# Two feed-forwards whose high and low token parts share one 512-column product, and an expert stage with one more buffer, a regrouped gather and a branch that stands later

## The chip, the cores and the metric

The kernel runs on one core of a Trainium2 chip. The metric is the device time of one launch in microseconds (us); lower is better. A profiled execution leaves a trace, whose span is the time from its first to its last instruction.

## The reference, cut to what matters

256 tokens of width 1024 pass through two blocks, all in 32-bit floats. The part that matters here:

```python
def swiglu(x, w_gate, w_up, w_down):                      # hidden width 2816, twice in the first block
    return (jax.nn.silu(x @ w_gate) * (x @ w_up)) @ w_down

x = x + FFN_HALF * swiglu(rms_norm(x, norm_ffn1[l]), ffn1_gate[l], ffn1_up[l], ffn1_down[l])
...                                                       # stick-breaking attention and RWKV-7
x = x + FFN_HALF * swiglu(rms_norm(x, norm_ffn2[l]), ffn2_gate[l], ffn2_up[l], ffn2_down[l])
...                                                       # second block: context, differential attention, Fourier
def hier_moe(h, w_rg, b_rg, w_re, b_re, w1, w3, w2):      # 4 groups of 4 experts, the best 2 of one group
    g_sel = jnp.argmax(t @ w_rg + b_rg, axis=-1)
    ...
    y = (jax.nn.silu(t @ w1e) * (t @ w3e)) @ w2e          # for each expert, times its gate
```

## The kernel before, in words

The program has five stages: feed-forward 1, the mixing of the first block, feed-forward 2, the projections and attention of the second block, and the 16 experts. Engines run their own queues in program order: PE (TensorE) multiplies, ACT (ScalarE) and DVE (VectorE) work between, POOL does small things, SP issues the weight loads. Outside the stretches marked `manual_schedule` a scheduler decides the order in each queue by priority; inside them it is the order in which the code is written.

**Feed-forwards.** To keep the accuracy of 32-bit floats with fast products, every weight and every token value is split into a high and a low part. A load brings 1 MB (`raw`, 128 x 2048); `split_w` makes from each half of it `hi` (ACT, L262) and `lo` (DVE, L263), three buffers of each. `swiglu` runs over 11 chunks of 256 hidden columns. In each, `fm256` forms the gate and then the up product: for two halves f of 128 columns and 8 pieces k of the width, three products into the same 256 columns of a PSUM bank: high weights by high tokens (L226), high weights by low tokens (L227), low weights by high tokens (L228). A chunk has 4 x 8 such threes, both feed-forwards 704. The bank with both halves is read once: silu (L618), multiplication (L619), splitting (L518, L519). Then `down256` multiplies the chunk before with 24 products of 512 columns (L403, L404, L407) into four banks that collect the result. Banks of the kind `pa` are four, taken in turn.

**Experts.** `x_add`, `x_turn`, `x_high` and `logits` form the residual, its transpose, the high part of the normalized tokens and the router's 20 logits for each block b of 128 tokens. `x_low(b)` (DVE) makes the low parts, and `pick(b)` (eight small DVE operations) chooses the group and its two experts. `rank` products number the tokens of each expert, `one_hot` makes selection matrices, and `gather(p)` multiplies them with the tokens for a pair p of experts (`gat`, L1799); DVE writes the result scaled to `xe` (L1800). There are 8 pairs; each has three products with 4 MB of weights: `gate(p)`, `up(p)` and `down(p)`, all at L1832. The order on PE is gate(p), down(p-1), up(p), sometimes gather(p+1), `back(p)`, the adding back of pair p-1 to the tokens, and the transposes `hidden_T(p)` (`eT`). Behind gate(0) `places()` forms the gates' slots (`gsl`).

The weights of the experts are 96 loads of 1 MB. `load_rows` deals them out in turn over 13 buffers: 5 `rawa`, 4 `raw`, 4 `rawb`. SP issues them in one queue and waits for a buffer to come free. An expert has 64 places; if any token finds none, `overflow()` computes all experts densely in a branch (`tc.If`, L1904) that every engine must decide. Here no token overflows, and the branch is skipped. SP's way around the branch waits until all loads issued so far have landed. In the kernel before the branch stands behind pair 6, and the loads (7,0), (6,2) and (7,1) are issued ahead of it, where (p,i) is the product i (0 gate, 1 up, 2 down) of pair p; (7,2) follows it.

Of the kernel before, what the change touches and what calls it, by code (L numbers as in the profile page):

```python
# [33 lines left out]
def constants():  # L34
# [57 lines left out]
    nm=17, m1=4,  # L92
# [5 lines left out]
    ffn={"4": 16, "2": 11, "1": 2, "m": 12},  # L98
    mid={"r4": 9, "r2": 6, "r1": 7, "rm": 16, "v4": 3, "s4": 6, "sm": 6, "gm": 4, "m2": 2, "mm": 2, "pm": 4, "cm": 4, "c1": 2},
    blk={"4": 9, "2": 5, "1": 7, "m": 25}, att={"4": 6, "2": 9},  # L100
    moe={"4": 4, "xe": 2, "oh": 2, "h": 3, "1": 2, "m": 16}, raws=(5, 4, 4))
# [16 lines left out]
def _body(tc, nc, es, I, out, dbg, stop, R):  # L118
# [36 lines left out]
    def t4(name, dt=F32, tag=None):  # L155
        return alloc("4", 1024, name, dt, tag)

# [127 lines left out]
    def fm256(w, c0, h, l, nk=8, wk=None, ps=None):  # L285
# [8 lines left out]
        return ps  # L294

# [150 lines left out]
    H = [cp.tile([128, 1024], F32R, name=f"H{i}") for i in range(4)]  # L446
    K4 = [cp.tile([128, 1024], F32, name=f"K{i}") for i in range(4)]
# [36 lines left out]

    def hl(name, tag=None):
        if tag == "H":
            h, l = H[0:2], H[2:4]
        else:
            h = [t4(name + "h", F32R, tag) for _ in range(2)]
            l = [t4(name + "l", F32R, tag) for _ in range(2)]  # L490
        v = lambda ts: (lambda k: ts[k // 4][:, 256 * (k % 4):256 * (k % 4) + 256])
        return v(h), v(l)
# [5 lines left out]
    def trans_split(xn, sc, bias, name, tag=None):  # L498

        h, l = hl(name, tag)  # L500
# [14 lines left out]
        return h, l  # L515
# [5 lines left out]
    def lead(xs, src, nk, n, sc, bias=None, evac=None, fk=0):  # L521


        h, l = hl("", "H")
# [65 lines left out]
        return h, l, lambda: picker(ws, n), lambda: picker([ws1, split_w(raw1, 1)], n)  # L590

    def swiglu(xs, g, wg, wu, wd, pre=None):

        if pre:
            h, l, w0, w1 = pre
            yield
        else:
            xn = normed(xs, "xn")
            yield
            h, l = trans_split(xn, g, None, "hT")  # L600
# [9 lines left out]
        for j in range(nch):  # L610
            if j == 2 and c1dma:
                c1dma()
            pg = fm256(wg, 256 * j, h, l, 8, w0)
            pu = fm256(wu, 256 * j, h, l, 8, w1)
            w0 = w1 = None
# [120 lines left out]
    def context_steps():  # L736
# [3 lines left out]
        h, l = hl("", "H")  # L740
# [29 lines left out]
    def context_values(n):  # L770
        h, l = hl("", "H")
# [17 lines left out]
    M["hT"], M["lT"], w0, w1 = lead(x, [I["w_in"][:, c:c + 256] for c in FIRST], 8, 256, gain("nm"), None, M["evac"])  # L789
# [594 lines left out]
    hT, lT, *w0 = lead(x, [w2i[512 * i:512 * i + 512, 1024:1536] for i in range(2)], 4, 512, col(sc1), col(sh1), M["evac"])  # L1384
# [86 lines left out]
    heads = [t4("heads") for _ in range(2)]  # L1471
# [14 lines left out]
    def attention():  # L1486
# [47 lines left out]
        def turn(n):  # L1534
# [6 lines left out]
            h_, l_ = t4("aTh", F32R), t4("aTl", F32R)  # L1541
# [30 lines left out]
    yF = [t4("yF") for _ in range(2)]  # L1572
# [87 lines left out]
    yh, yl = hl("y2", "H")  # L1660
# [15 lines left out]
    pl = pa("lgp")  # L1676
    route = tc.manual_schedule(engines={mybir.EngineType.DVE, mybir.EngineType.Activation})
# [38 lines left out]
    def logits(b):  # L1716
        for k in range(8):
            mm(pl[:, 32 * b:32 * b + 20], xT[b][:, 128 * k:128 * k + 128], wr[:, k, :], start=k == 0, stop=k == 7)
# [7 lines left out]
    def pick(b):  # L1726
        DVE.scalar_tensor_tensor(L[:, b], pl[:, 32 * b:32 * b + 20], rsx[:, b:b + 1], rbias, op0=OP.mult, op1=OP.add)
        v = L[:, b].rearrange("p (g e) -> p g e", g=5)
        vi, vj = v[:, :, :, None].to_broadcast([128, 5, 4, 4]), v[:, :, None, :].to_broadcast([128, 5, 4, 4])
        gt, eq = (t1(n)[:, 0:80].rearrange("p (g i j) -> p g i j", g=5, i=4) for n in ("gt", "eq"))  # L1730
        tri = C("tri").rearrange("p (i j) -> p i j", i=4)[:, None].to_broadcast([128, 5, 4, 4])
# [4 lines left out]
        DVE.tensor_reduce(rk[:, b], gt, axis=AX.X, op=OP.add)  # L1736
        DVE.tensor_scalar(sel[:, b], rk[:, b, 0], 0.0, None, op0=OP.is_equal)
# [342 lines left out]
```

## Time and profile before

| | |
|---|---|
| Time, median of 3 runs (lowest to highest) | 1179.94 us (1179.67 to 1182.61) |
| The profiled execution's own time | 1180.25 us |
| Its span | 1178.5 us, so 1.75 us lie around it |
| PE busy | 1108.8 us, 94% of the span |
| DVE, ACT busy | 621.2 us (53%), 477.3 us (40%) |
| Moved from memory | 262.98 MB, 223 GB/s in the mean |

PE is busy nearly everywhere; the loads are light at first (about 190 GB/s in the feed-forwards) and at the limit near the end (420 GB/s). A shorter time can so come from less work on PE in the first part and from an earlier, denser stream of loads in the last. Matmuls overlap in the records: the cost of one is the distance from its start to the next one's start, not its recorded duration.

### The profile page before, as it was taken

To read this page: it belongs to the slowest core of one execution; us is meant where nothing else is said; L and a number is where in the kernel's file an instruction comes from. 1 tells how busy PE (TensorE), PEld (TensorE's weight loads), DVE (VectorE), ACT (ScalarE), POOL (GpSimd) and SP (SyncE) were. 2 spreads that over 40 slices of the span, in tenths; PEclk is the share of its full clock that TensorE was granted. 3 is DMA by queue.
4 is the path that set the end of the run, shared out by engine and by line. 5 is a ranking of instruction groups with operands and counts; after the bars stand their busy time and mean duration, and the time that the engine had idled before them with its cause. 6 is when DMAs were issued, how large, how long until landed. Compare 5 with 4: busy or idle time off the path is not lost. (4 is left out here: it accounts for less than half of the span.)

```text
span 1178.5 us, 17991 instructions
## 1 busy us (share of the span) xinstructions
PE 1108.8 (94%) x7527; PEld 870.1 (74%) x7527; DVE 621.2 (53%) x928; ACT 477.3 (40%) x711; POOL 60.7 (5%) x106
## 2 busy tenths in 40 slices
PE   6999999998988999999999999999899799999976
PEld 6999997887756888999998688888898534343432
DVE  4545545556976556455445865666656603232314
ACT  5444444476643355444444445555544300100002
POOL 1000001000330001000000100000000200000000
PEclk9999999999988999999999999999999799999988
DMA  9855654453557548555556454214285399999984
GB/s 338 275 191 179 198 180 158 157 169 112 179 197 261 197 139 304 195 179 185 175 191 218 153 179 160 72 55 152 96 327 210 145 366 419 421 420 420 421 354 175
DMA packets 119538, 262.98 MB, mean 223 GB/s; under 512 B 6873, under 2 KB 83802, under 8 KB 105242
## 3 DMA queue, kind: packets, MB, share of 16 engines
q1 hardware_dynamic: 118506, 258.88, 60.7%
q0 software_dynamic: 656, 2.36, 0.6%
q8 instruction: 61, 1.00, 0.3%
q10 hardware_dynamic: 288, 0.52, 0.1%
q14 instruction: 27, 0.22, 0.1%
HBM read 260.70 MB, written 1.05 MB: 222 GB/s over the span
## 5 line engine op out<-in xcount | busy, mean ns | idle before, releaser
L263 DVE TENSOR_TENSOR lo<-raw,hi 128x1024 fp32r<-128x1024 f32 x243 | 297.2, 1224 | 285.9 <-ACT hi L262 285.5
L262 ACT ACTIVATE hi<-raw 128x1024 fp32r<-128x1024 f32 x246 | 260.6, 1060 | 318.2 <-PE pj L227 203.3
L227 PE MATMUL pj<-H,hi 128*128 128x256 f32 x752 | 212.4, 283 | 4.1 <-issue 4.1
L226 PE MATMUL pj<-H,hi 128*128 128x256 f32 x752 | 216.2, 288 | 0.0
L228 PE MATMUL pj<-H,lo 128*128 128x256 f32 x752 | 212.4, 282 | 0.4 <-POOL lo L263 0.4
L226 PEld LDWEIGHTS pj<-H,hi 128*128 128x128 f32 x752 | 142.8, 190 | 8.5 <-issue 4.5
L228 PEld LDWEIGHTS pj<-H,lo 128*128 128x128 f32 x752 | 143.0, 190 | 5.2 <-issue 4.5
L227 PEld LDWEIGHTS pj<-H,hi 128*128 128x128 f32 x752 | 142.7, 190 | 1.3 <-issue 0.5
L228 PE MATMUL pj<-hTh,lo 128*128 128x256 f32 x352 | 99.4, 283 | 0.1
L227 PE MATMUL pj<-hTl,hi 128*128 128x256 f32 x352 | 99.2, 283 | 0.0
L226 PE MATMUL pj<-hTh,hi 128*128 128x256 f32 x352 | 99.1, 283 | 0.0
L227 PEld LDWEIGHTS pj<-hTl,hi 128*128 128x128 f32 x352 | 67.3, 192 | 1.3 <-DVE hTl L509 0.8
L226 PEld LDWEIGHTS pj<-hTh,hi 128*128 128x128 f32 x352 | 67.2, 192 | 1.2 <-ACT hTh L508 0.8
L228 PEld LDWEIGHTS pj<-hTh,lo 128*128 128x128 f32 x352 | 67.4, 192 | 0.3 <-DVE lo L263 0.3
L1881 DVE TENSOR_TENSOR yf<-yacc,K 128x512 f32<-128x512 f32 x16 | 11.0, 691 | 104.7 <-PE yacc L1832 82.5
L404 PE MATMUL acc<-lo,hTh 128*128 128x512 f32 x160 | 63.1, 394 | 0.0
L403 PE MATMUL acc<-hi,hTh 128*128 128x512 f32 x160 | 62.7, 392 | 0.0
L407 PE MATMUL acc<-hi,hTl 128*128 128x512 f32 x160 | 49.9, 393 | 0.0
L1832 PE MATMUL pu<-rawa,xe 128*64 128x512 f32 x160 | 45.3, 605 | 0.0
L1864 ACT ACTIVATE hT<-eT 128x512 f32<-128x512 f32 x8 | 4.8, 597 | 91.6 <-PE eT L1863 91.6
L1832 PE MATMUL pg<-raw,xe 128*64 128x512 f32 x128 | 35.8, 595 | 0.0
L1832 PE MATMUL yacc<-rawb,hT 128*64 128x512 f32 x128 | 35.5, 592 | 0.0
(496 smaller groups left out, 1895.2 us busy)
## 6 DMA issues: line engine op xcount, KB each, us to landing
raw<-in_w_in_dram SPq DMA_DIRECT2D x43, 1024.0 KB, 5.1
raw<-in_ffn_up_dram SPq DMA_DIRECT2D x22, 1024.0 KB, 5.2
raw<-in_ffn_down_dram SPq DMA_DIRECT2D x22, 1024.0 KB, 4.9
raw<-in_ffn_gate_dram SPq DMA_DIRECT2D x21, 1024.0 KB, 5.2
rawa<-in_w_exp_up_dram SPq DMA_DIRECT2D x20, 1024.0 KB, 19.2
raw<-in_w_exp_gate_dram SPq DMA_DIRECT2D x16, 1024.0 KB, 14.1
rawb<-in_w_exp_down_dram SPq DMA_DIRECT2D x16, 1024.0 KB, 17.5
raw<-in_w_mod_dram SPq DMA_DIRECT2D x15, 1024.0 KB, 5.0
```

Of the source, the lines that this page charges most:

```text
L226: mm(o, l[0], r[0], start=first, stop=False)
L227: mm(o, l[0], r[1], start=False, stop=False)
L228: mm(o, l[1], r[0], start=False, stop=last)
L262: ACT.activation(hi, r, AF.Copy)
L263: low = lambda: (sub or DVE).tensor_tensor(lo, r, f32(hi), op=OP.subtract)
L403: mm(ps[b][n], hh, wh[:, s_], start=first and f == 0, stop=False)
L404: mm(ps[b][n], hh, wl[:, s_], start=False, stop=False)
L407: mm(ps[b][n], ll, wh[:, s_], start=False, stop=last and f == 1)
L1832: mm(o[halves[u]], l[:, 64 * u:64 * u + 64], r[u], start=first, stop=last, tile_position=(0, 64 * u))
L1864: ACT.activation(t, ps, AF.Copy)
L1881: tt(part(yf, n), yaccs[p][n], part(g2b, n), op=OP.mult)
```

## The change

The feed-forwards place the high and the low tokens behind one another in one tile (`H`, or two `t8` tiles), so that one product of 512 columns with the high weights (L308) gives both halves of a whole bank; a product of 256 columns with the low weights (L311) adds to its first half. The two halves of the bank are then added by ACT (copy) and DVE (addition), for each f apart, before silu and the multiplication. Ahead of the experts the picks of both blocks become one with operations twice as wide, `x_low(1)` moves behind the first one-hots, `gather(0)` goes over four banks, high parts first, then low, and ACT shares the scaling; PE's order there is the written one. The tiles K0 and K1 become one that serves as a 14th buffer for expert weights. The loads (7,2) are issued ahead of the branch, and the branch stands behind hidden_T of pair 7. The last `down` does its first half of the data in the common order and its second half by column half. `few` in the skipped branch loads from ACT's queue.

```diff
-    raws=(5, 4, 4))
+    raws=(5, 4, 4, 1))
@@ load_rows
+        elif i == sum(n) - 1:
+            raw = K01
+    def fm128s(w, c0, hl2, wk=None):
+        wk = wk() if wk else cols(w, c0, 256, 0, 8)
+        for f in range(2):
+            ps, s_ = pa("pj"), slice(128 * f, 128 * f + 128)
+            for k in range(8):
+                wh, wl = wk(k)
+                high = lambda: mm(ps, wh[:, s_], hl2(k), start=k == 0, stop=k == 7)
+                if k < 7:
+                    high()
+                mm(ps[:, 0:256], wl[:, s_], hl2.h(k), start=False, stop=False)
+                if k == 7:
+                    high()
+            yield ps[:, 0:256], ps[:, 256:512]
@@ swiglu
-            pg = fm256(wg, 256 * j, h, l, 8, w0)
-            pu = fm256(wu, 256 * j, h, l, 8, w1)
-            ACT.activation(hp, pg, AF.Silu)
-            tt(hp, hp, pu, op=OP.mult)
-            split2(hT[0], hT[1], hp)
+            for s_, (a, b) in zip(sides, fm128s(wg, 256 * j, hl2, w0)):
+                t = t1("gs")
+                ACT.activation(t, a, AF.Copy)
+                tt(t, t, b, op=OP.add)
+                ACT.activation(hp[:, s_], t, AF.Silu)
+            for s_, (a, b) in zip(sides, fm128s(wu, 256 * j, hl2, w1)):
+                t, o = t1("us"), hp[:, s_]
+                ACT.activation(t, a, AF.Copy)
+                tt(t, t, b, op=OP.add)
+                tt(o, o, t, op=OP.mult)
+                split2(hT[0][:, s_], hT[1][:, s_], o)
@@ routing
     x_low(0)
-    pick(0)
-    x_low(1)
-    pick(1)
+    pick()
@@
     for b in range(2):
         one_hot(b, 0, 4)
+    x_low(1)
@@ gather
+        if p == 0:
+            pss = pc2("gat") + pc2("gat")
+            for i in range(2):
+                for k in range(8):
+                    sums(pss[k // 2], k, i, i == 0 and k % 2 == 0, i == 1)
+            for k in range(8):
+                if k % 2:
+                    ACT.activation(g(k), half(pss[k // 2], k), AF.Identity, bias=sh2p[:, k:k + 1], scale=sc2p[:, k:k + 1])
+                else:
+                    DVE.tensor_scalar(g(k), half(pss[k // 2], k), sc2p[:, k:k + 1], sh2p[:, k:k + 1], op0=OP.mult, op1=OP.add)
+            for b in range(2):
+                one_hot(b, 4, 12)
+            return
@@ down
         if p == 7:
-            steps.sort(key=lambda v: v[1])
+            steps[4:] = [(2, 0), (3, 0), (2, 1), (3, 1)]
@@ the pairs
             hTs[p] = hidden_T(hps[p], alloc("h", 512, "hT", F32, ""))
-            if p == 6:
-                ahead.update({k: fetch(*k) for k in ((7, 0), (6, 2), (7, 1))})
+            if p == 7:
+                ahead[7, 2] = fetch(7, 2)
                 overflow()
```

On PE, in the first chunk of feed-forward 1, a stretch of the queue reads so before (`H_78`, `H_79` are high tokens, `H_80`, `H_81` low ones, `hi` and `lo` the weights):

```order
L226 MATMUL pj<-H_78,hi 128x256
L227 MATMUL pj<-H_80,hi 128x256
L228 MATMUL pj<-H_78,lo 128x256
L226 MATMUL pj<-H_79,hi 128x256
L227 MATMUL pj<-H_81,hi 128x256
L228 MATMUL pj<-H_79,lo 128x256
```

and so now:

```order
L308 MATMUL pj<-H,hi 128x512
L311 MATMUL pj<-H,lo 128x256
L308 MATMUL pj<-H,hi 128x512
L311 MATMUL pj<-H,lo 128x256
L308 MATMUL pj<-H,hi 128x512
```

Of each three rows two remain, with as many columns in all.

On DVE, from the end of the logits to the first results of the gather, before (`H_81<-x_72` is x_low(1), `m` the picks, `oh` the one-hots; the six rows of each pick between its first and last are left out):

```order
L1727 SCALAR_TENSOR_TENSOR L<-lgp,rsx,rbias 128x20
...
L1738 SCALAR_TENSOR_TENSOR m_8820<-rk,sel 128x16
L1713 SCALAR_TENSOR_TENSOR H_81<-x_72,rsx,H_79 128x512 x2
L1727 SCALAR_TENSOR_TENSOR L<-lgp,rsx,rbias 128x20
...
L1738 SCALAR_TENSOR_TENSOR m_8820<-rk,sel 128x16
L1773 TENSOR_TENSOR oh<-c_67,rank 128x256 x2
L1780 COPY pr_8933<-rank 128x32
L1800 TENSOR_SCALAR xe<-gat,sc2p,sh2p 128x256 x2
```

and now:

```order
L1765 SCALAR_TENSOR_TENSOR L<-lgp,rsx,rbias 128x20 x2
L1771 TENSOR_TENSOR gt<-L 128x160
...
L1778 SCALAR_TENSOR_TENSOR m_8504<-rk,sel 128x16 x2
L1811 TENSOR_TENSOR oh<-c_67,rank 128x256 x2
L1750 SCALAR_TENSOR_TENSOR H<-x_72,rsx,H 128x512 x2
L1819 COPY pr_8609<-rank 128x32
L2035 RECIPROCAL den<-den 128x2
L1850 TENSOR_SCALAR xe<-gat,sc2p,sh2p 128x256 x4
```

x_low(1) has moved from between the picks to behind the one-hots, one pick is gone, and the reciprocal of the gates now stands ahead of the gather's results.

On SP, the end of the queue of loads before (the rows of the skipped branch are left out):

```order
L245 DMA rawb<-in_w_exp_up_dram 128x2048 x3
L245 DMA rawa<-in_w_exp_up_dram 128x2048
L1903 TENSOR_LOAD novi
L1904 COMPARE_AND_BRANCH
...
L1904 UNCONDITIONAL_BRANCH x2
L1903 ISA x2
L245 DMA rawa<-in_w_exp_down_dram 128x2048 x4
```

and now:

```order
L250 DMA rawa<-in_w_exp_up_dram 128x2048
L250 DMA raw<-in_w_exp_up_dram 128x2048 x3
L250 DMA raw<-in_w_exp_down_dram 128x2048
L250 DMA rawb<-in_w_exp_down_dram 128x2048 x3
L1960 TENSOR_LOAD novi
L1961 COMPARE_AND_BRANCH
```

The last four loads of weights have moved from behind the branch to ahead of it.

## Rows read from the trace of the kernel before

**Rows 1.** The page's first line.

```profile
span 1178.5 us, 17991 instructions
```

**Rows 2.** Busy time by stretch, in feed-forward 1: us, then PE, PEld, DVE, ACT, POOL, clock, DMA.

```profile
100.00:150.00 50.00, 50.00 (x357) 47.11 (x356) 24.79 (x25) 21.97 (x24) 0.00 (x0) 1.00 0.58 190
```

**Rows 3.** Timeline of PE in one chunk: start us, duration us, engine, line, operation.

```profile
99.80 0.28 PE L226 MATMUL pj<-H,hi 128*128 128x256 f32 x1
...
105.14 0.39 PE L403 MATMUL acc<-hi,hTh 128*128 128x512 f32 x1
...
110.61 0.28 PE L226 MATMUL pj<-H,hi 128*128 128x256 f32 x1
```

**Rows 4.** Groups by shape: busy us, mean ns of one, then idle time and its releasers.

```profile
L263 DVE TENSOR_TENSOR lo<-raw,hi 128x1024 fp32r<-128x1024 f32 x243 | 297.2, 1224 | 285.9 <-ACT hi L262 285.5 <-PE scp L1495 0.2
L262 ACT ACTIVATE hi<-raw 128x1024 fp32r<-128x1024 f32 x246 | 260.6, 1060 | 318.2 <-PE pj L227 203.3 <-PE acc L407 53.5 <-PE qkp L380 24.8
...
L579 ACT ACTIVATE H<-trp,vec 128x256 fp32r<-128x256 f32 x16 | 6.2, 488 | 7.2 <-PE trp L542 7.2
```

**Rows 5.** Timeline of DVE at the routing.

```profile
922.35 0.24 DVE L1727 SCALAR_TENSOR_TENSOR L<-lgp,rsx,rbias 128x20 f32<-128x20 f32 x1 [0.80 <-PE lgp L1718]
...
924.16 2.14 DVE L1713 SCALAR_TENSOR_TENSOR H<-x,rsx,H 128x512 fp32r<-128x512 f32 x2
...
927.94 0.17 DVE L1738 SCALAR_TENSOR_TENSOR m<-rk,sel 128x16 fp32r<-128x16 f32 x1
928.59 0.75 DVE L1773 TENSOR_TENSOR oh<-c,rank 128x256 fp32r<-128x256 f32 x2 [0.47 <-PE rank L1768]
```

**Rows 6.** Timeline of PE from the gather to up(0).

```profile
929.16 3.76 PE L1799 MATMUL gat<-oh,H 128*128 128x256 f32 x16 [0.60 <-DVE oh L1773]
...
936.24 3.21 PE L1832 MATMUL pg<-rawa,xe 128*64 128x512 f32 x6 [0.64 <-DVE xe L1800]
...
947.36 1.95 PE L1810 MATMUL gsl<-ghl,oh 128*128 128x4 f32 x16
...
949.82 0.64 PE L1832 MATMUL pu<-rawa,xe 128*64 128x512 f32 x1
```

**Rows 7.** Timeline of SP: loads of expert weights.

```profile
917.00 0.56 SPq L245 DMA_DIRECT2D rawb<-in_w_exp_down_dram  x1
942.37 4.60 SPq L245 DMA_DIRECT2D rawa<-in_w_exp_down_dram  x3
...
1147.75 2.04 SPq L245 DMA_DIRECT2D rawa<-in_w_exp_down_dram  x4
```

**Rows 8.** Busy time by stretch among the experts; the last two numbers are the DMA's share and GB/s.

```profile
960.00:970.00 10.00, 10.00 (x49) 3.45 (x49) 0.00 (x0) 1.19 (x2) 0.00 (x0) 1.00 1.01 422
...
1131.00:1140.00 9.00, 9.00 (x34) 2.95 (x33) 0.00 (x0) 0.11 (x1) 0.00 (x0) 0.79 1.02 419
1140.00:1147.00 7.00, 7.00 (x36) 2.60 (x34) 0.00 (x0) 0.49 (x1) 0.00 (x0) 1.00 0.65 267
1147.00:1152.00 5.00, 5.00 (x26) 1.75 (x24) 2.58 (x4) 1.23 (x2) 0.00 (x0) 1.00 0.62 228
```

**Rows 9.** The branch's line: duration ns least/median/most, first and last start us.

```profile
L1904 PEldq COMPARE_BRANCH  x1: 6164/6164/6164, 1124.1 to 1124.1; - x1
L1904 DVEq COMPARE_BRANCH  x1: 72/72/72, 1124.6 to 1124.6; - x1
```

**Rows 10.** Timeline of PE: a down product; then the end of pair 7.

```profile
998.05 3.60 PE L1832 MATMUL yacc<-rawb,hT 128*64 128x512 f32 x16
1001.48 3.60 PE L1832 MATMUL yacc<-rawa,hT 128*64 128x512 f32 x16
...
1153.44 0.44 PE L1826 MATMUL oht<-ident,oh 128*128 128x128 f32 x2
...
1155.57 0.63 PE L1863 MATMUL eT<-ident,hp 128*128 128x128 f32 x4
...
1160.13 5.36 PE L1832 MATMUL yacc<-rawa,hT 128*64 128x512 f32 x22 [0.46 <-DMA rawa<-in_w_exp_down_dram]
```

More of the change, by code (lines that the diff above doesn't have):

```diff
@@ L156, in t4, with t8 @@
         return alloc("4", 1024, name, dt, tag)
+    def t8(name, dt=F32):
+        return alloc("8", 2048, name, dt, "")
     def t2(name, dt=F32, tag=None):
@@ L788, in _body @@
     FIRST = (0, 256)
-    M["hT"], M["lT"], w0, w1 = lead(x, [I["w_in"][:, c:c + 256] for c in FIRST], 8, 256, gain("nm"), None, M["evac"])
+    M["hT"], M["lT"], M["hl"], w0, w1 = lead(x, [I["w_in"][:, c:c + 256] for c in FIRST], 8, 256, gain("nm"), None, M["evac"])
     for b in range(2):
@@ L1469, in _body @@
     run(gv)
-    heads = [t4("heads") for _ in range(2)]
+    two = lambda t: [t[:, 0:1024], t[:, 1024:2048]]
+    heads = two(t8("heads"))
     tl = lambda t, h: t[h // 4][:, 256 * (h % 4):256 * (h % 4) + 256]
@@ L1571, in _body @@
     sga = [t4("sga") for _ in range(2)]
-    yF = [t4("yF") for _ in range(2)]
+    yF = two(t8("yF"))
     def fourier():
@@ L1724, in _body, with pick @@
     by4 = lambda t: t.rearrange("p b (g e) -> p b g e", g=4)
[L1726 to L1731, printed above, removed]
+    def pick():
+        for b in range(2):
+            DVE.scalar_tensor_tensor(L[:, b], pl[b][:, 0:20], rsx[:, b:b + 1], rbias, op0=OP.mult, op1=OP.add)
+        v = L.rearrange("p b (g e) -> p (b g) e", g=5)
+        n = [128, 10, 4, 4]
+        vi, vj = v[:, :, :, None].to_broadcast(n), v[:, :, None, :].to_broadcast(n)
+        gt, eq = (t1(n)[:, 0:160].rearrange("p (g i j) -> p g i j", g=10, i=4) for n in ("gt", "eq"))
+        tri = C("tri").rearrange("p (i j) -> p i j", i=4)[:, None].to_broadcast(n)
         tt(gt, vj, vi, op=OP.is_gt)
@@ L1792, in gather, with sums @@
             xe[p + u] = lambda k, u=u: t[:, 256 * k + 128 * u:256 * k + 128 * u + 128]
+        g = lambda k: t[:, 256 * k:256 * k + 256]
+        half = lambda ps, k: ps[:, 256 * (k % 2):256 * (k % 2) + 256]
+        def sums(ps, k, i, first, last):
+            for b in range(2):
+                mm(half(ps, k), (xnh, xnl)[i][b][:, 128 * k:128 * k + 128], oh[b][:, 128 * p:128 * p + 256],
+                   start=first and b == 0, stop=last and b == 1, skip_group_check=p == 0)
+        if p == 0:
[8 more added lines that the diff above has]
+                    DVE.tensor_scalar(g(k), half(pss[k // 2], k), sc2p[:, k:k + 1], sh2p[:, k:k + 1], op0=OP.mult, op1=OP.add)
+            for b in range(2):
+                one_hot(b, 4, 12)
+            return
         for k in range(8):
@@ L1795, in gather @@
                 ps = pa("gat")
-            o, s_ = ps[:, 256 * (k % 2):256 * (k % 2) + 256], slice(128 * k, 128 * k + 128)
-            for i, w in enumerate((xnh, xnl)):
-                for b in range(2):
-                    mm(o, w[b][:, s_], oh[b][:, 128 * p:128 * p + 256], start=i + b == 0, stop=i + b == 2)
-            DVE.tensor_scalar(t[:, 256 * k:256 * k + 256], o, sc2p[:, k:k + 1], sh2p[:, k:k + 1], op0=OP.mult, op1=OP.add)
-            if p == 0 and k in (1, 3):
-                one_hot(k // 2, 4, 12)
+            for i in range(2):
+                sums(ps, k, i, i == 0, i == 1)
+            DVE.tensor_scalar(g(k), half(ps, k), sc2p[:, k:k + 1], sh2p[:, k:k + 1], op0=OP.mult, op1=OP.add)
     def places():
```

69 lines of the change are left out of this document (39 added, 30 removed).

## The prediction, made before the changed kernel ran

> **What bounds the kernel now.** I began with the span [rows 1] and the busy time by stretch. In feed-forward 1 PE is busy 50.00 of 50 us at full clock, DVE 24.8 and ACT 22.0 [rows 2]: only what PE issues counts there. PE's price is the distance between starts, since the recorded durations (280 and 390 ns) overlap: 45 products of 256 columns stand between 99.80 and 105.14, so 118.7 ns each, and 24 of 512 columns between 105.14 and 110.61, so 227.9 ns each [rows 3].
>
> The last 250 us are limited otherwise. In 960 to 970 the DMA share is 1.01 at 422 GB/s [rows 8]: a load of 1.049 MB every 2.48 us, and the products follow the data. This stream can't start before buffers come free. The last load into a free buffer is issued at 917.00, the next at 942.37, after gate(0) has read the first buffers [rows 7]; in between the stream rests. So what ends before gate(0), namely logits, picks, ranks and the gather [rows 5, 6], delays the whole stream. At the end SP lets the last four loads wait until the branch is decided: 1140 to 1152 shows DMA shares of 0.65 and 0.62, and the four go out at 1147.75 [rows 7, 8]. The last half of down(7) waits for them and starts at 1160.13 [rows 10]. What follows it (last additions, normalization, output) is left as it is.
>
> **Feed-forwards.** Three products of 256 columns, 356.1 ns, become one of 512 and one of 256, 227.9 + 118.7 = 346.6 ns. Per three 9.5 ns go, times 704: **-6.7 us**. As many columns pass as before, so what is saved is one start of a product. The bounds: 0, if the start's price belongs to the columns' second segment, since the 512 columns are now read from two places; and -13.4, if the short product behind a long one also loses its start, because its weights load under the longer one. Both prices in rows 3 are of uniform runs, and the mixed one lies nearest to the plain sum.
>
> The Trainium skill ("TensorE: Matmul & The Clock Gate", section "Back-to-back issue gap") gives about N/2.4 + 2.5 ns for an issue of N columns. By it, as an estimate, the three would cost 327.5 ns and the pair 325.0, and the change would bring 1.8 us instead of 6.7; here a 256-column product took 118.7 ns where that formula gives 109.2, so the trace doesn't agree and I go by the trace.
>
> What is added stands beside PE. Per chunk there are four copies on ACT and four additions on DVE of 256 columns, about 0.49 us each by the nearest row [rows 4], and silu, multiplication and split go by halves: some 3 us more per engine in a chunk of about 17 us, where each is idle about half the time [rows 2]. The tight place is the second half of the up weights: its `hi` and `lo` buffers come free when gate's f = 1 is at its half, splitting takes 1.06 + 1.22 us [rows 4], and two ACT operations (copy, silu of f = 0) may now stand ahead, about 1 us. One f of gate lasts 8 x 0.347 = 2.8 us, so the split would be ready within a few tenths of its need. I count 0; above that is the slow rival.
>
> **Routing and gather.** The two picks take about 1.8 us each (922.35 to 924.16) with x_low(1), 2.14 us, between them [rows 5]. One pick of double width costs something between 1.8 us (only starts cost) and 3.2 (all is width, beside what is now shared); its operations have 80 columns at most, so I take 2.3, near the lower end. The masks then end at 924.8 instead of 927.94 + 0.17, and the first one-hots, two ranks and two comparisons later, let the gather start at 926.3 instead of 929.16: -2.8 us. Before, gate(0) began at 936.24, the gsl products at 947.36 and up(0) at 949.82 [rows 6]. Now 16 high products take 3.76 us (the row that has the low clock of this place), 16 low ones 16 x 118.7 ns = 1.9 us; x_low(1), moved behind the one-hots, is done by about 928.7, before the low products begin at 930.1. The data scaled, gate(0) can start at about 932, 32 products at 3.43 us per 16 [rows 10] take 6.86 us, and the slots 2.46 (947.36 to 949.82). So up(0) stands at about 941.3, **8.5 us** earlier. For the stream the point that counts is the first freed `rawa` buffer, halfway through gate(0): 926.3 + 5.66 + 3.43 = 935.4 instead of 942.37: **-7.0 us**. The reciprocal of the gates, which now stands ahead of xe on DVE, waits for the chain on POOL; I have it ready at about 929.3 and count nothing. If it is late, gate(0) is late by as much.
>
> **14th buffer.** One more load goes out in the rest before 942.37 and leaves the stream's dense part: **-2.5 us** (2.48). It is worth 0 only if the stream were not the limit behind it.
>
> **Loads ahead of the branch.** Lost between 1140 and 1152 are (1 - 0.65) x 7 + (1 - 0.62) x 5 = 4.35 us [rows 8], which go: **-4.3 us**. Together the stream is 13.8 us earlier: (7,2) lands at 1146.3 instead of 1160.13, and (7,1), four loads ahead, at 1136.3.
>
> **The branch behind pair 7.** Here something is given back. PE needs 6164 ns for the skipped branch, DVE 72 [rows 9]. Before, this lay in a place where the data set the pace; now it stands between hidden_T(7) and down(7), where the data will have landed. The chain: (7,1) at 1136.3; the second half of up(7), 3.43, 1139.8; the adding back and eT, from 1153.44 to 1155.57 + 0.63 [rows 10], 2.76 us, 1142.5; the branch 6.3, 1148.8. PE's idle time costs clock as well: behind the branch, from 1131 to 1140, PE was granted 0.79 [rows 8], so 9 x 0.21 = 1.9 us were lost. down(7) takes 6.86 + 1.9 and ends at 1157.6; before it ended at 1160.13 + 5.36 = 1165.5 [rows 10]. As the two column halves now end close together, one DVE operation of about 0.6 us more stands behind the last product. The expert part so gains 7.9 - 0.6 = **7.3 us**, of the stream's 13.8.
>
> The Trainium skill ("Runtime: NRT & Kernel Launch", section "Instruction fetch mechanics") says that a taken branch whose target lies outside the window of fetched instructions has to fetch it by DMA. That the engine with the long body pays 6164 ns and the one with the short body 72 agrees with it, and by it the later place doesn't make the skip shorter; it is only no longer covered.
>
> **Sum.** 6.7 + 7.3 = 14.0 us. 1178.5 - 14.0 = 1164.5 span; with the 1.75 us around it (1180.25 - 1178.5) 1166.3. The median shown is 0.3 us below the profiled execution: **1166 us**.
>
> **The rivals.** *A, the skip is short (0.12).* The DMA queues are quiet once the last loads have landed, so the fetch may be quicker than under full load, where the 6164 ns were taken. With a skip of 2 us and full clock down(7) starts at 1144.5, its second half follows 3.43 us later, and it ends at 1151.4: 13.5 us instead of 7.3, so 1160, and less if the mixed products save more too. For it: no row prices a skip beside a quiet memory. Against: the stream is still dense while PE branches at 1142.5 (it ends at 1146.3).
>
> *B, the wide product brings nothing (0.13).* Two segments, or a fixed price per column, leave 356 ns a three: 1173. For it: no row has a product that reads two segments. Against: the 512-column products of rows 3 do show 9.5 ns less.
>
> *C, the stream's earlier start is lost (0.10).* The reciprocal waits for POOL, or ACT's part of the scaling is late, and gate(0) starts 5 to 7 us later than I have it: 1171 to 1173.
>
> *D, slower (0.13).* In a chunk, PE waits for the split of the up weights' second half, behind copy and silu on ACT. 14.0 / 22 chunks = 0.64 us: from that wait on per chunk the gain is gone. With 1.2 us, about one copy, one silu and a bit, 22 x 1.2 = 26 us go and the time is 1192. For it: a margin of tenths. Against: ACT and DVE idle half the chunk [rows 2], and a delay that ends within the chunk's reserve is not repeated. I give half of this case to waits below or about 0.64, near no change.
>
> **Range and chances.** My forecast has 0.52. A reaches down to about 1158 with double savings in the feed-forwards; B and C up to 1173. 1158 to 1174 leaves out D and extremes, under 2 in 10. 0.3%, 3.5 us, is about what a measurement of this kernel tells from no change. Faster 0.87 (forecast, A, B, C), same 0.06 and slower 0.07 (both D).
>
> **What would show it.** Right: pairs of L308 and L311 at 347 ns, chunks shorter by about 0.3 us, and PE never waiting for `hi` or `lo` there; up(0) near 941, with the stream's restart at 935; a DMA share of 1.0 until (7,2) has landed at 1146; PE's COMPARE_BRANCH of about 6 us at 1142, and a clock below 1 behind it. Wrong: pairs at 356 ns (B), at 337 (the lower bound); a wait of gate(0) for xe with DVE at the reciprocal (C); a short branch (A); waits of L308 for `hi`, with ACT at `gs` (D). The rest of the program keeps its order; a change of several us in the mixing or the attention would be something that I have not seen.

## The result, and the profile after

The changed kernel took 1168.09 us (median of 4 runs, 1166.33 to 1170.21) beside 1179.81 us (1179.59 to 1182.61) of the kernel before: ratio 0.9875, 95% interval 0.9847 to 0.9903. The profiled execution took 1166.33 us, and its span is 13.9 us shorter than the 1178.5 of [rows 1]. The page's first lines:

```profile
span 1164.6 us, 16858 instructions
...
PE 1099.5 (94%) x6823; PEld 834.5 (72%) x6823; DVE 656.5 (56%) x1050; ACT 513.0 (44%) x847; POOL 61.9 (5%) x106
```

PE has 704 products fewer (and as many weight loads), and DVE and ACT 35 us more work each. A sum over the whole says nothing yet of where the time went, so I cut the span at PE's own products. FF1 and FF2 reach from the first to the last start of a down product of the feed-forward, the mixing lies between them. The first two chunks of each feed-forward lie ahead of its first down product, so those of feed-forward 1 count in the stage before FF1 and those of feed-forward 2 in the mixing. The expert part begins with the first transposition of x for the router and ends with the last product of down(7). Its first row before, and then its rows on PE after: the first transposition, the gather, gate(0), up(0), the second half of up(7), and down(7), which ends at 1147.20 + 4.03 = 1151.23. Its end before is the last row of [rows 10], 1160.13 + 5.36:

```profile
915.25 1.47 PE L1697 MATMUL trp<-ident,x 128*128 128x128 f32 x12
```

```profile
912.65 1.47 PE L1734 MATMUL trp<-ident,x 128*128 128x128 f32 x12
...
923.67 5.75 PE L1837 MATMUL gat<-oh,H 128*128 128x256 f32 x32 [0.60 <-DVE oh L1811]
929.35 7.09 PE L1889 MATMUL pg<-rawa,xe 128*64 128x512 f32 x32
...
938.83 0.64 PE L1889 MATMUL pu<-rawa,xe 128*64 128x512 f32 x1
...
1131.93 3.65 PE L1889 MATMUL pu<-raw,xe 128*64 128x512 f32 x14 [1.33 <-SPq L1961]
...
1142.55 1.08 PE L1889 MATMUL yacc<-raw,hT 128*64 128x512 f32 x1 [4.27 <-PEq L1961]
...
1147.20 4.03 PE L1889 MATMUL yacc<-rawb,hT 128*64 128x512 f32 x17
```

Stage by stage, in us, from the two traces (the last row is the whole):

| | before | after | difference |
|---|---|---|---|
| up to FF1 | 37.70 | 36.80 | -0.9 |
| FF1 | 162.46 | 159.94 | -2.5 |
| mixing | 283.88 | 286.83 | +3.0 |
| FF2 | 164.87 | 162.47 | -2.4 |
| projections, attention | 266.34 | 266.61 | +0.3 |
| expert part | 250.24 | 238.58 | -11.7 |
| output | 13.01 | 13.37 | +0.4 |
| span | 1178.5 | 1164.6 | -13.9 |

So the sum of 14.0 came out, but by other terms than I had: less from the feed-forwards, more from the experts, and a loss in a stage that I had not counted.

**Feed-forwards.** The timeline of PE in a chunk of the changed kernel, start and duration in us; the last row here is the first down product behind the chunk's pairs, and below it stands the same product of the kernel before:

```profile
103.14 0.40 PE L423 MATMUL acc<-hi,hTh 128*128 128x512 f32 x1
...
108.59 0.40 PE L308 MATMUL pj<-H,hi 128*128 128x512 f32 x1
108.83 0.28 PE L311 MATMUL pj<-H,lo 128*128 128x256 f32 x1
108.94 0.39 PE L308 MATMUL pj<-H,hi 128*128 128x512 f32 x1
109.17 0.28 PE L311 MATMUL pj<-H,lo 128*128 128x256 f32 x1
109.29 0.40 PE L308 MATMUL pj<-H,hi 128*128 128x512 f32 x1
...
119.73 0.40 PE L423 MATMUL acc<-hi,hTh 128*128 128x512 f32 x1
```

```profile
122.00 0.39 PE L403 MATMUL acc<-hi,hTh 128*128 128x512 f32 x1
```

The chunk's 32 pairs take 11.14 us (108.59 to 119.73), 348 ns each, where 32 threes took 11.39 (110.61 [rows 3] to 122.00), 356. The mixed form has no price of its own far from the uniform ones. PE stayed busy without a gap, with DVE and ACT at 31 and 27 of 50 us instead of the 25 and 22 of [rows 2], so the new work lies beside it:

```profile
100.00:150.00 50.00, 50.00 (x268) 43.08 (x267) 30.84 (x43) 27.10 (x42) 0.00 (x0) 1.00 0.58 189
```

**Experts.** The loads of SP, and the busy time by stretch behind their restart and at the end (the last two numbers are the DMA's share and GB/s):

```profile
917.70 0.44 SPq L250 DMA_DIRECT2D rawb<-in_w_exp_down_dram  x1
933.03 0.80 SPq L250 DMA_DIRECT2D rawa<-in_w_exp_down_dram  x2
936.46 6.37 SPq L250 DMA_DIRECT2D rawa<-in_w_exp_up_dram  x3
...
1117.01 5.31 SPq L250 DMA_DIRECT2D rawb<-in_w_exp_down_dram  x3
```

```profile
943.00:948.00 5.00, 4.44 (x22) 1.67 (x20) 1.08 (x2) 0.37 (x1) 0.00 (x0) 1.00 0.96 364
...
1130.00:1135.00 5.00, 3.67 (x18) 1.05 (x14) 0.00 (x0) 0.00 (x0) 0.00 (x0) 1.00 1.02 423
1135.00:1140.00 5.00, 3.27 (x16) 2.23 (x14) 3.47 (x6) 0.60 (x1) 0.00 (x0) 1.00 0.95 390
1140.00:1145.00 5.00, 2.46 (x6) 0.85 (x8) 0.00 (x0) 0.00 (x0) 0.00 (x0) 0.74 0.10 38
```

The gap of [rows 8] before the end is gone: the DMA share stays near 1.0 until (7,2) has landed. PE begins to skip the branch while these loads still run. The branch's line (instructions with their shortest, median and longest duration in ns, first and last start in us):

```profile
L1961 SPq EVENT_SEMAPHORE  x8: 17/17/17, 1126.9 to 1141.9; - x8
...
L1961 PEldq COMPARE_BRANCH  x1: 4287/4287/4287, 1137.9 to 1137.9; - x1
```

SP's eight releases behind the branch, the last at 1141.9, stand where the loads have landed. PE's skip ends at 1142.2, and only then down(7) begins, at a clock of 0.74 in its stretch, so that it takes 8.7 us (1142.55 to 1151.23).

### The profile page after: what moved, and what is told of

Same layout as the page of the kernel before. It is cut to its first block, busy times and chain, and to the rows that moved or that the text cites. A ratio compares the mean times of both kernels' runs of the same rounds, so it can differ in the third digit from the quotient of the medians.

```text
span 1164.6 us, 16858 instructions
## 1 busy us (share of the span) xinstructions
PE 1099.5 (94%) x6823; PEld 834.5 (72%) x6823; DVE 656.5 (56%) x1050; ACT 513.0 (44%) x847; POOL 61.9 (5%) x106
## 5 line engine op out<-in xcount | busy, mean ns | idle before, releaser
L308 PE MATMUL pj<-H,hi 128*128 128x512 f32 x352 | 122.1, 396 | 0.4 <-DVE H L599 0.4
L308 PE MATMUL pj<-hT,hi 128*128 128x512 f32 x352 | 122.0, 394 | 0.5 <-DVE hT L538 0.5
L229 PE MATMUL pj<-H,hi 128*128 128x256 f32 x400 | 117.6, 294 | 0.0
L231 PE MATMUL pj<-H,lo 128*128 128x256 f32 x400 | 113.6, 284 | 0.0
L230 PE MATMUL pj<-H,hi 128*128 128x256 f32 x400 | 113.6, 284 | 0.0
L311 PE MATMUL pj<-hT,lo 128*128 128x256 f32 x352 | 91.6, 281 | 0.0
L311 PE MATMUL pj<-H,lo 128*128 128x256 f32 x352 | 91.5, 281 | 0.0
L229 PEld LDWEIGHTS pj<-H,hi 128*128 128x128 f32 x400 | 76.9, 192 | 7.5 <-issue 4.4
L230 PEld LDWEIGHTS pj<-H,hi 128*128 128x128 f32 x400 | 76.9, 192 | 0.5 <-issue 0.5
L308 PEld LDWEIGHTS pj<-hT,hi 128*128 128x128 f32 x352 | 63.6, 188 | 13.3 <-DVE hT L538 1.5
L308 PEld LDWEIGHTS pj<-H,hi 128*128 128x128 f32 x352 | 64.1, 190 | 12.4 <-DVE H L599 0.8
L311 PEld LDWEIGHTS pj<-H,lo 128*128 128x128 f32 x352 | 66.8, 190 | 3.9
L311 PEld LDWEIGHTS pj<-hT,lo 128*128 128x128 f32 x352 | 66.2, 188 | 4.1
L647 ACT ACTIVATE gs<-pj 128x256 f32<-128x256 f32 x44 | 16.9, 384 | 44.3 <-PE pj L308 44.2
```

Of the source, the lines that this page charges most:

```text
L229: mm(o, l[0], r[0], start=first, stop=False)
L230: mm(o, l[0], r[1], start=False, stop=False)
L231: mm(o, l[1], r[0], start=False, stop=last)
L308: high = lambda: mm(ps, wh[:, s_], hl2(k), start=k == 0, stop=k == 7)
L311: mm(ps[:, 0:256], wl[:, s_], hl2.h(k), start=False, stop=False)
L647: ACT.activation(t, a, AF.Copy)
```

## The experiments

Twelve experiments follow, in three groups of four; a group shares its chip and its runs of the kernel before. All stage times below are from the profiled executions, cut as above. "Clock lost" is worked out from the mixing's rows of 10 us, as the sum of (1 - granted clock) x 10. In the expectations "theory 1" and "rival" are those of the run at hand; "theory 2" is always the same: that the new form of the feed-forwards lowers the clock in the mixing.

| kernel | ratio to before (95%) | FF1 | mixing | clock lost | FF2 | expert part |
|---|---|---|---|---|---|---|
| before | | 162.46 | 283.88 | 6.8 | 164.87 | 250.24 |
| changed | 0.9875 (0.9847 to 0.9903) | 159.94 | 286.83 | 10.2 | 162.47 | 238.58 |
| 1 feed-forwards alone | 0.9986 (0.9966 to 1.0006) | 159.93 | 289.62 | 11.9 | 162.47 | 251.12 |
| 2 experts alone | 0.9910 (0.9879 to 0.9940) | 162.49 | 283.04 | 6.8 | 164.44 | 238.55 |
| 3 branch behind gate(7) | 0.9920 (0.9889 to 0.9951) | 159.94 | 282.31 | 6.8 | 162.47 | 246.11 |
| 4 no branch | 0.9806 (0.9776 to 0.9836) | 159.93 | 285.55 | 10.2 | 162.47 | 233.45 |
| 5 changed again | 0.9869 (0.9840 to 0.9899) | 159.93 | 285.67 | 10.2 | 162.47 | 238.45 |
| 6 13 buffers | 0.9904 (0.9872 to 0.9937) | 159.93 | 285.42 | 10.2 | 162.47 | 242.46 |
| 7 branch behind pair 6 | 0.9888 (0.9860 to 0.9917) | 159.93 | 290.50 | 13.6 | 162.47 | 239.41 |
| 8 gate(7), own buffer | 0.9840 (0.9811 to 0.9870) | 159.93 | 287.84 | 12.0 | 162.47 | 232.33 |
| 9 feed-forward 1 old | 0.9869 (0.9848 to 0.9891) | 162.49 | 285.33 | 12.0 | 162.47 | 239.11 |
| 10 before again | 1.0002 (0.9985 to 1.0020) | 162.45 | 289.86 | 13.7 | 164.86 | 248.63 |
| 11 experts again | 0.9901 (0.9875 to 0.9926) | 162.46 | 283.29 | 8.5 | 164.31 | 240.06 |
| 12 old gather | 0.9937 (0.9911 to 0.9964) | 159.93 | 287.06 | 12.0 | 162.47 | 246.95 |

**1. Feed-forwards alone.** The picks, the gather, PE's order there, the buffers, the last down, the branch and the queue of `few` as before; the main cuts of the edit:

```diff
-    moe={...}, raws=(5, 4, 4, 1))
+    moe={...}, raws=(5, 4, 4))
...
-    pick()
+    pick(0)
+    x_low(1)
+    pick(1)
...
-            if p == 7:
-                ahead[7, 2] = fetch(7, 2)
+            if p == 6:
+                ahead.update({k: fetch(*k) for k in ((7, 0), (6, 2), (7, 1))})
                 overflow()
```

> The feed-forwards of the changed kernel with the expert part, the routing and the 13 buffers of the kernel before. Theory 1: a pair saves 8 to 9.5 ns, both feed-forwards 5.5 to 6.5 us in the profile, and that is the gain of the whole (-5 to -6.5 us) unless the clock falls in the mixing; how often it falls there is left to chance and not to the change. Theory 2: the mixing loses 2.8 us to a lower clock whenever the feed-forward before it is shorter or the tokens lie in the new tiles, so the whole gains only 2.5 to 3.5 us, and the profile shows a granted clock of about 0.8 between 257 and 297 us again.

FF1 and FF2 are 2.5 and 2.4 us shorter than before, yet the whole is not measurably faster (median 1180.26 beside 1181.51 us), and the mixing of its trace took 289.62 us. Every run has its span and mean granted clock listed, and span x (1 - clock) is an estimate of the time that a clock below 1 costs in it. It is 32.6 us in the mean of these 12 runs (standard error 0.8) and 28.6 in the 17 of the kernel before (0.7), while the span less this time is 1146.1 and 1151.5 us. So the saving of some 5 us is there in the runs too, and a lower clock takes 4.0 us of it back. By itself this spoke for theory 2.

**2. Experts alone.** The loop over the chunks in the old form:

```diff
-            for s_, (a, b) in zip(sides, fm128s(wg, 256 * j, hl2, w0)):
...
+            pg = fm256(wg, 256 * j, h, l, 8, w0)
+            pu = fm256(wu, 256 * j, h, l, 8, w1)
...
+            ACT.activation(hp, pg, AF.Silu)
+            tt(hp, hp, pu, op=OP.mult)
+            split2(hT[0], hT[1], hp)
```

> The changed kernel with the old loop over the feed-forward's chunks (three products of 256 columns), all else as changed. Theory 1: the expert part gains 11 us by itself, since the stream is denser at its restart and the skip costs 4.3 us there: -10 to -12 us against before, about 1168 to 1170. Rival, the forecast as it stood: -7 to -8 us, about 1172, and the rest of what was measured is from elsewhere.

1170.31 us beside 1181.51, and the expert part 238.55 as in the changed kernel: theory 1. Most of the measured gain is the experts'.

**3. Branch behind gate(7).**

```diff
             gate(p)
+            if p == 7:
+                ahead.update({k: fetch(*k) for k in ((6, 2), (7, 1), (7, 2))})
+                overflow()
...
-            if p == 7:
-                ahead[7, 2] = fetch(7, 2)
-                overflow()
```

> The changed kernel with the branch behind gate(7), and the loads (6,2), (7,1), (7,2) issued ahead of it. Theory 1: PE's skip lies partly in its waits for data: gate(7) ended at 1117.5 in the changed kernel's trace, then skip 6.2, down(6) 7.0, up(7) 6.9, adding back and transposes 2.8, down(7) 6.9 give 1147.5 instead of 1151.2, so -2 to -4 us against the changed kernel. Rival: behind the branch DVE or ACT waits until SP has passed it, which is when the last load has landed (1142), so that the adding back of pair 6 and all behind it is late: 0 to +5 us against the changed kernel.

The rival: the expert part got 7.5 us longer. PE lost only 2.70 us at the skip, but DVE's yf of pair 6 waited for SP. DVE's row, then PE's behind it:

```profile
1137.56 1.29 DVE L1938 TENSOR_TENSOR yf<-yacc,K 128x512 f32<-128x512 f32 x2 [29.28 <-SPq L1961]
```

```profile
1117.15 8.78 PE L1889 MATMUL yacc<-rawa,hT 128*64 128x512 f32 x32 [2.70 <-PEq L1961]
...
1138.97 0.80 PE L1946 MATMUL scat<-yh,back 128*128 128x512 f32 x1 [5.80 <-ACT yh L1939]
```

The product scat needs yh and yh needs yf, so PE stood idle 5.80 us more. The clock fell with both waits of PE, which is a further part of the loss:

```profile
1115.00:1120.00 5.00, 2.85 (x10) 1.21 (x12) 0.00 (x0) 0.16 (x1) 0.00 (x0) 0.81 1.01 415
...
1135.00:1140.00 5.00, 1.03 (x2) 0.59 (x3) 2.34 (x4) 1.23 (x2) 0.00 (x0) 0.52 0.18 75
```

The tile yf is of a kind with four buffers, and `few`, into which the skipped branch loads, is of the same kind. Whether that is the cause of DVE's wait is asked in 8.

**4. No branch.** The dense path for tokens without a place is left out.

```diff
                 ahead[7, 2] = fetch(7, 2)
-                overflow()
```

> The changed kernel without the branch: the dense path for tokens that find no place is left out (none needs it with these inputs). Theory 1: what the branch costs in its later place is the skip of 4.3 us and the low clock behind it, 1.8 us: -5 to -6 us against the changed kernel, down(7) then being limited by its data (1142 + 3.4). Rival: the skip is covered by the landing of (7,2) at 1141.9 anyway, so that less than 2 us go.

Theory 1: the expert part is 5.1 us shorter. down(7) stands 1.3 us behind the start of eT (1136.75 to 1138.07) where the changed kernel has 4.9 (1137.64 to 1142.55), which is 3.6, and it runs 7.1 us at full clock instead of 8.7. It wasn't held by data.

**5. Changed again.** No edit.

> The changed kernel once more, to have it on the same chip as the three below. Theory 1 (the mixing's length is a matter of chance, since its waits are short and the clock falls behind some of them in some executions): FF1, FF2 and the expert part of the profile as in its first trace to within 0.5 us (159.9, 162.5, 238.6), the mixing anywhere between 282 and 290. Theory 2 (the change itself makes the mixing slower): the mixing at 286 or above.

All stages agree with the first trace to 0.2 us but the mixing (285.67, -1.2) and the projections and attention (267.96, +1.4). It doesn't tell the two theories apart.

**6. 13 buffers.**

```diff
-    moe={...}, raws=(5, 4, 4, 1))
+    moe={...}, raws=(5, 4, 4))
```

> The changed kernel with 13 buffers. Theory 1 (the stream sets the time until up(7)): 2.5 us more in the expert part, 241.1 instead of 238.6. Rival (the restart of the stream and the skip at its end set the time, one load more or less ahead is taken up): less than 0.5 us more.

3.9 us more, so theory 1 and more than its 2.5. Counted from the first transposition, the second half of up(7) starts at 222.4 instead of 219.3, 3.1 later, and down(7) takes 9.5 us, 0.9 more:

```profile
1144.46 9.54 PE L1889 MATMUL yacc<-rawa,hT 128*64 128x512 f32 x32 [4.22 <-PEq L1961]
```

**7. Branch behind pair 6.**

```diff
-            if p == 7:
-                ahead[7, 2] = fetch(7, 2)
+            if p == 6:
+                ahead.update({k: fetch(*k) for k in ((7, 0), (6, 2), (7, 1))})
                 overflow()
```

> The changed kernel with the branch behind pair 6 and the loads (7,2) behind the branch, as before. Theory 1: the later branch hardly paid, since what the stream gained at its end went into the skip and the clock behind it: the expert part is 239.5 to 240.5, that is 1 to 2 us more than changed. Rival: the whole 4.3 us that the stream loses there come back: 242 to 243.

Only 0.8 to 1.0 us more, the lower edge of theory 1. The gap is back (DMA shares 0.65 and 0.47), but down(7) runs straight through at full clock behind it:

```profile
1130.00:1135.00 5.00, 5.00 (x26) 1.68 (x24) 0.00 (x0) 0.60 (x1) 0.00 (x0) 1.00 0.65 269
1135.00:1140.00 5.00, 5.00 (x26) 1.68 (x24) 2.67 (x4) 1.26 (x2) 0.00 (x0) 1.00 0.47 154
```

So the later branch, with its loads ahead, gained almost nothing: the skip and the clock behind it took what the denser stream gave.

**8. Branch behind gate(7), own buffer.** The third experiment, with `few` in a tile of the kind of xe. The cut of the edit that differs from the third:

```diff
+        few = [alloc("xe", 2048, "few", F32, ""), 0]
...
-            t = t4("few")
+            few[1] ^= 1
+            t = few[0][:, 1024 * few[1]:1024 * few[1] + 1024]
```

> The branch behind gate(7), as in the third experiment, and the tile into which the skipped branch loads taken from the two xe buffers instead of the four that yf uses, so that DVE's yf behind the branch needs none of SP's releases. Theory 1: PE's skip then lies in its waits for data and what follows it is PE's own work: the expert part ends 3 us earlier than changed, at 235 to 236. Rival (the wait behind the branch is not due to that tile, or the low clock behind the skip costs as much as the skip): 238 or more.

Theory 1, and more than it: 6.1 us less than changed in the expert part, 1163.22 us beside 1166.86 of the fifth (same chip), though its trace had the longer mixing of the two. 0.8 us of the 6.1 it had by gate(0) already, which began 15.9 us behind the first transposition instead of 16.7. yf now waits only for PE, and behind the branch only PE itself waits. Its skip takes 6192 ns, but the wait is 2.66 us: PE's queue came to the branch at 1114.2, while products of gate(7) that had been issued ahead ran until 1118.0.

```profile
1120.69 7.09 PE L1889 MATMUL yacc<-rawa,hT 128*64 128x512 f32 x32 [2.66 <-PEq L1963]
```

```profile
1127.01 1.49 DVE L1938 TENSOR_TENSOR yf<-yacc,K 128x512 f32<-128x512 f32 x2 [15.14 <-PE yacc L1889]
```

```profile
1115.00:1120.00 5.00, 3.03 (x16) 0.72 (x11) 0.00 (x0) 0.60 (x1) 0.00 (x0) 1.00 1.01 413
1120.00:1125.00 5.00, 4.31 (x20) 1.78 (x22) 0.00 (x0) 0.00 (x0) 0.00 (x0) 1.00 1.01 415
```

The clock stayed at 1.00 behind a wait as long as the 2.70 us of the third experiment. Of the 13.8 us between the two (246.11 and 232.33), 11.2 arise behind the skip, from the start of down(6) to the end of down(7) (36.6 and 25.4 us), by DVE's wait and the lower clock of the third. The other 2.5 were there ahead of it, 0.9 of them by gate(0), and have nothing to do with the tile. This is the fastest version that still has the branch; its ratio's interval overlaps with that of the changed kernel, the stages don't.

**9. Feed-forward 1 old.** The old loop where the stage is the first, the new one where it is the second.

```diff
+            if not P.get("ffn2"):
+                pg = fm256(wg, 256 * j, h, l, 8, w0)
+                pu = fm256(wu, 256 * j, h, l, 8, w1)
...
```

> The changed kernel with feed-forward 1 in the old form (three products of 256 columns) and feed-forward 2 in the new one. In the profiles so far the mixing between them took 283.0 and 283.9 us behind the old form, 282.3 to 290.5 (mean 286.7 of eight) behind the new. Theory 2 (what the new form saves in feed-forward 1 is given back by a lower clock in the mixing): FF1 162.5 and the mixing 283 to 284, the whole within 1 us of the changed kernel. Theory 1 (the clock in the mixing is chance and has nothing to do with the form): the mixing anywhere between 282 and 290, and the whole 2.5 us longer than the changed kernel in the median.

FF1 is 162.49, the mixing 285.33: neither the 283 to 284 of theory 2 nor far from it. In the whole it equals the changed kernel (0.9869), but the interval reaches 2.5 us to either side, which is the difference that was asked for. Not decided by this one.

**10. Before again.** No edit to the kernel before.

> The kernel before once more, for another trace of its mixing. Theory 2: 283 to 284 us, with the granted clock at 1.00 between 60 and 80 us behind feed-forward 1, where it was 0.9 in seven of eight traces of the new form. Theory 1: between 282 and 290, with the clock below 1 there as often as not.

The mixing took 289.86 us, 6 more than in the first trace of the same instructions, and the clock was below 1 where theory 2 wants 1.00. The place, first in the first trace of the kernel before, then in this one, then in the changed kernel: one row of PE's timeline and the row of a stretch of 10 us that begins about there.

```profile
268.04 0.70 PE L849 MATMUL lora<-tw,w2a 64*128 64x256 f32 x2 [1.49 <-ACT sw L850]
```

```profile
267.00:277.00 10.00, 8.96 (x72) 8.63 (x73) 4.53 (x6) 4.30 (x8) 0.00 (x0) 1.00 0.38 120
```

```profile
268.27 0.70 PE L849 MATMUL lora<-tw,w2a 64*128 64x256 f32 x2 [1.50 <-ACT sw L850]
```

```profile
269.00:279.00 10.00, 10.00 (x71) 10.00 (x72) 2.97 (x5) 3.33 (x5) 0.00 (x0) 0.83 0.31 100
```

```profile
264.64 0.74 PE L885 MATMUL lora<-tw,w2a 64*128 64x256 f32 x2 [1.50 <-ACT sw L886]
```

```profile
263.60:273.60 10.00, 8.96 (x60) 8.58 (x61) 3.16 (x4) 3.53 (x7) 0.00 (x0) 0.83 0.31 107
```

PE waits 1.5 us for ACT in all three. Behind it the clock fell in two of the three. Theory 2, in the form in which it was put, is out: the old form too can have the lower clock. The odds are another question. In the two rows of 10 us between 60 and 80 us behind feed-forward 1 the clock was below 1 in eight of the nine traces with the new form of it and in one, this one, of the five with the old.

**11. Experts again.** As the second.

> The changed kernel with both feed-forwards in the old form, once more, for a third trace of the mixing behind the old form and beside the one before it. Theory 2: mixing 283 to 284; the whole 2 us longer than the changed kernel was against its own kernel before, or less. Theory 1: mixing 282 to 290, the whole 5 us longer.

Mixing 283.29 (as theory 2 has it, and within theory 1), expert part 240.06, the whole 0.9901. The expert part is 1.5 us longer than in the second experiment by PE's skip, which took 5484 ns here and 3962 there, in the same program and the same place. With the second experiment: the changed kernel less its feed-forwards stands at 0.990 to 0.991, with them at 0.987 to 0.988, so they bring about 4 us of the whole (0.0033 x 1180), with an uncertainty nearly as large. By the granted clocks it is clearer: the 12 runs of the second and of this experiment lost an estimated 24.4 us to the clock and the 10 of the changed kernel (with the fifth, not all on one chip) 23.9, each with a standard error of 0.7 to 0.8, and the span less this time is 1144.9 and 1141.4 us. So 3.5 us are the feed-forwards' here, and no lower clock is seen with them.

**12. Old gather.** The two picks, x_low(1) between them, the gather over two banks at a time, as before; all else as changed.

```diff
-    pick()
+    pick(0)
+    x_low(1)
+    pick(1)
...
-            pss = pc2("gat") + pc2("gat")
```

> The changed kernel with the picks, x_low(1), the gather and the order on PE there as before; feed-forwards, buffers and the branch as changed. Theory 1 (what ends before gate(0) delays the whole stream): the expert part 6.5 to 8 us longer than changed, 245 to 246.5, nearly all of it in the restart of the loads 6.7 us later. Rival (the stream takes it up, since the 14 buffers and the loads ahead of the branch leave it slack): under 3 us longer.

Theory 1 in the sum, and a little above it: 8.4 us more. But the first load behind the rest goes out only 4.3 us later than changed (24.6 us behind the first transposition, instead of 20.4), and the second half of up(7) is 7.6 later (226.9 instead of 219.3), since the next loads are later by more: the last of the three that follow goes out 36.1 us behind the first transposition (943.90 + 7.18), where the changed kernel has 30.2 (936.46 + 6.37):

```profile
939.63 1.99 SPq L250 DMA_DIRECT2D rawa<-in_w_exp_down_dram  x2
943.90 7.18 SPq L250 DMA_DIRECT2D rawa<-in_w_exp_up_dram  x3
```

## Why the prediction held, and where it was off

1166 was forecast and 1168.09 measured, inside the range. The mechanisms were mostly right, but four terms were mis-sized, and that their sum came out so close is luck.

**The pair.** Forecast 346.6 ns, 9.5 less than three products. 32 pairs took 11.14 us in feed-forward 1 where 32 threes took 11.39, and 11.23 where 11.50 in feed-forward 2, so a pair saves 8.0 to 8.2 ns and the 704 pairs 5.7 us instead of 6.7. FF1 and FF2 are 4.93 us shorter (2.53 + 2.40), since they hold 18 of the 22 chunks; the other four lie in the stages ahead of them. The mechanism was right, and rival B is out by its own condition: FF1 took 162.45 to 162.49 us in the old form and 159.93 or 159.94 in the new, in every trace. The formula of the Trainium skill ("TensorE: Matmul & The Clock Gate", section "Back-to-back issue gap"), which the page gives for an isolated product and from which I had estimated 1.8 us, gives too small a saving here. Rival D's wait, PE standing for `hi` or `lo`, didn't come: PE was busy 50.00 of 50 us, and all 18 of these chunks took 11.14 or 11.23 us.

**The routing.** From the first transposition on: the gather starts 2.9 us earlier (13.91 to 11.02; forecast 2.8), up(0) 8.4 (34.57 to 26.18; forecast 8.5), the restart 6.7 (27.12 to 20.38; forecast 7.0). The reciprocal was no obstacle: gate(0) starts at 929.35, right behind the gather's last product and without a wait, so rival C is out.

**The stream.** The second half of up(7) started 219.3 us behind the first transposition; the forecast's 1136.3 was 221.05. These 1.8 us are more than I had. Behind the restart the stream is denser: in the 20 us there the DMA share was 0.81, 0.96, 0.74, 1.01 before, of which the third stretch is the row of before below (clock 0.86, up(0) slowed; that its buffers so came free late is my reading), and 0.81, 0.99, 0.96, 1.01 after, worth (0.48 - 0.23) x 5 = 1.25 us. I had taken the restart to shift as it was. The rest of the 1.8 is not accounted for; the 14th buffer alone, taken at 2.5 us, was worth 3.1 at this point (6).

```profile
952.40:957.40 5.00, 5.00 (x22) 1.64 (x20) 0.00 (x0) 0.00 (x0) 0.00 (x0) 0.86 0.74 274
```

**The skip.** I took 6164 ns, the row under full load, and gave rival A, a shorter one beside a quiet memory, 0.12. It was between the two: 4287 ns. This is a term that was mis-sized by 2.0 us, and the last section shows with what it goes. That the later place doesn't make the skip shorter, as I had argued, was wrong. The clock behind it was as forecast (down(7) 8.7 us, forecast 8.76). That the skip gives back what the branch's later place brings was right. By the forecast's own sum it gave back more than that: 4.3 us came in and 5.9 went (13.8 - 7.9), a net loss of 1.6. Undone (7), the place is worth a gain of 0.8 to 1.0 us of the 11.7 in the expert part. The gather (12: 8.4 us) and the buffer (6: 3.9) make the rest; with 0.8 to 1.0 for the place the three come to 13.1 to 13.3 instead of 11.7, so they aren't quite additive. The order of the last down and the queue of `few` were not undone by themselves. The DVE operation more behind the last product, taken at 0.6 us, shows as 0.4 in the output. The 1.8 us of the stream and the 2.0 of the skip are the 3.8 us by which the expert part gained more than forecast (11.7 instead of 7.9).

**The mixing.** "The rest of the program keeps its order" was right, and that it keeps its time was the step that failed. The mixing, nearly the same instructions in every kernel (the two chunks of feed-forward 2 in it are worth 0.5 us), took 282.3 to 290.5 us in 14 traces, and the length less the clock lost is 273 to 278 in all of them. In the pair of traces first compared, that made +3.0 us; with another trace of the kernel before it would have been -3.0. Whether the new feed-forward shifts the odds stays open: the mixing took 285.1 us in the mean of five traces behind the old form, 286.8 of nine behind the new, with a spread of 2 to 3 us in each. The clocks of all runs say two things. Beside the old expert part the new form loses 4.0 us more to the clock (1), beside the new one no more than the old form (2, 11). So the feed-forwards' 5.7 us are shown in their own stages; in the whole time 1.7 us (1: 0.0014 x 1180) to 4 us (2, 11) of them are seen.

The total was close because an expert part that gained 4 us more than forecast met a mixing that lost 3 and feed-forwards that gained 1 less. The mixing's 3 us hang on the two traces compared, so the agreement to 2 us is luck.

## What to carry to other kernels

A branch that is skipped costs what its slowest engine needs to get around it, less what that engine has still queued ahead of it and what it would wait for data anyway. Ahead of the last product it cost 5.1 us here (4); behind gate(7), with 3.85 us of products queued ahead and a stream that was the limit, it cost nothing that was seen (232.33 us in 8, 233.45 without a branch). What stood behind this branch and shared a kind of tile with what the branch would load waited for the loads of the whole queue (3); a tile of another kind took the wait away (8). Compare traces stage by stage before you believe a total: a sum can agree by errors that cancel, and a stage with short waits changed its length by 6 us between two executions of the same program (283.88 and 289.86 in the kernel before).

## What the runs showed of the hardware that was not expected

PE's skip was shorter where the last loads were landing. In the six traces with a DMA share of 1.0 all through it, it took 6164 ns ([rows 9]), 6052 (1), 6232 (3), 5972 (7), 6192 (8) and 6016 (10). In the seven in which the share fell to nothing within some 3 us, it took 4287 (changed), 3962 (2), 4467 (5), 4227 (6), 4322 (9), 3927 (12) and, against the rest, 5484 (11). The rows of three of them, the eighth, the second and the eleventh experiment:

```profile
L1963 PEldq COMPARE_BRANCH  x1: 6192/6192/6192, 1114.2 to 1114.2; - x1
```

```profile
L1954 PEldq COMPARE_BRANCH  x1: 3962/3962/3962, 1140.6 to 1140.6; - x1
```

```profile
L1954 PEldq COMPARE_BRANCH  x1: 5484/5484/5484, 1141.1 to 1141.1; - x1
```

DVE passed the same branch in 72 ns each time. The Trainium skill ("Runtime: NRT & Kernel Launch", section "Instruction fetch mechanics") states that a taken branch whose target lies outside the window of fetched instructions waits for a DMA fetch of it. The traces agree. Their DMA records hold the packets of a queue of the kind "instruction", 16 KB each; the changed kernel's page counts them:

```profile
q8 instruction: 55, 0.90, 0.3%
```

In all 13 traces with the branch a packet of this queue lands during PE's skip, and the skip ends 1.3 to 1.6 us behind the landing of the last one, in the long skip of the eleventh experiment too. What differs is when that packet starts, 3.4 to 3.8 us behind the skip's start in the six traces with the dense stream and 0.9 to 2.1 in the seven others; and in the eleventh it took 2.0 us itself, elsewhere 1.1 to 1.4. That q8 is PE's queue is my reading (6 packets fewer than before, with 1408 products and weight loads fewer on PE), and why the packet starts later beside the dense stream is not shown. No run here took the transfers away altogether.

The granted clock behind one and the same wait of 1.5 us stayed at 1.00 in one execution and fell in another, and with waits of 2.70 (3) and 2.66 us (8) in the same place it was 0.81 in the stretch of 5 us from 1115 in one and 1.00 in that from 1120 in the other. What decides it was not found.
